# Half of the attention weights turned by VectorE and DMA, and every engine in the order of the source

## The chip, the cores and the metric

One Trainium2 chip, one of its cores. The metric is the device time of one launch in microseconds (us). A profile is one more execution, recorded instruction by instruction. The engines: TensorE (PE in the profile, its weight loads PEld), VectorE (DVE), ScalarE (ACT), GpSimd (POOL), and SyncE (SP), which here only issues DMAs.

## The reference

One block of a hybrid encoder: 512 tokens of width 2048, all in float32. Cut to what matters here:

```python
mod = silu(c) @ w_cond + b_cond                       # shift, scale, gate
h = rms_norm(x) * (1 + scale) + shift
proj = h @ w_in                                       # 2048 x 7200
aq, ak, av, ag, gq, gk, gv, gg, lr_f, lr_b = split(proj)
# attention, 16 heads of 64; three dilated windows (128,1), (512,4), (2048,16),
# merged by their softmax denominators, a shared T5 bias on the logits
a_out = merged_attention(aq, ak, av, rel_bias) * silu(ag)
# gated linear attention, 4 heads, forward and backward scans summed
g_out = rms_norm(o_fwd + o_bwd) * gla_norm_gain * silu(gg)
x = x + gate * (concat(a_out, g_out) @ w_out)
return rms_norm(x) * final_gain
```

For one head the three windows merge into one softmax over all 512 keys, with one bias row by distance (it holds the log of how many windows contain a key). So P, the weights of a head, is a 512 x 512 matrix, made in four tiles of 128 queries x 512 keys. The product with the values needs it with the keys on the partitions: each tile has to be turned.

## The kernel before

Each float32 operand is split into a high part (rounded to the float32r that TensorE takes) and a low part (the rest). `three` sums three products: high by high, high by low, low by high. ScalarE makes the high part (`split_hi`, `act(hi, raw)`), VectorE the low one (`split_lo`, `tt(lo, raw, hi, subtract)`).

After a first stage (condition sums, norm, the value columns `sa` and the columns `sb`) the projection runs in units of 512 columns, in the order qk2, qk4, qk6, gk, gv0, gv1, ag0, ag1, gg0, gg1, o0 to o3. A unit has eight weight groups of 256 rows (512 KB each, tile `raw`, four buffers). A group is loaded two or three ahead and split one ahead (tiles `whi` and `wlo`, three buffers each). The unit has four PSUM tiles `ps_...`, out of five buffers, and each group gives six matmuls to each of them. The unit's progress is counted in ticks: three matmuls are a tick, 64 ticks a unit.

Beside a unit's matmuls runs side work, put at places that are shares of the ticks. In qk2, qk4, qk6 and gk this is `attention` of four heads (two pairs) each. For each of a head's four tiles of queries:

- `score`: two matmuls (PSUM `s`), on VectorE the sum with the bias row and the minimum (tile `p`), on ScalarE the exponential with the row sum, on VectorE the reciprocal of the sum (`st`), on POOL the scaling of `p`.
- `turn`: four TensorE transposes into PSUM `t`, then high part (ScalarE) and low part (VectorE) into `pt`.
- `values`, for two tiles (a half of the head's queries) together: eight matmuls with the value tiles `vv`, PSUM `o`; ScalarE copies one half (`oh`), VectorE adds the other into `cat`.

At the end of qk2, qk4 and qk6 `qk_evict` takes four PSUM tiles into the operands of the next four heads: `qs` and `ks` (high part by ScalarE, low part by VectorE, in each of two halves), `kl`, and DMAs that copy `ks` and `kl` to the other 64 partitions. It is written behind the unit's loop, ahead of the next unit.

Other side work are sums of 1024 columns on VectorE (`rawv` for a bias row of the values, `rawg` for the gate), each with a load of 512 KB. `SUMS_IN` says how many go into which unit.

TensorE executes in the order of the source. ScalarE, VectorE, POOL and SP are ordered by the framework's scheduler from the first `qk_evict` on; there the side work is marked urgent. Semaphores tie the engines together, and each engine takes its own list in order.

## Time and profile before

| | us |
|---|---|
| median of three runs | 958.55 |
| the three runs | 958.09, 958.55, 958.55 |
| the profiled execution | 959.9 |
| its span, first to last instruction | 957.9 |
| TensorE busy in the span | 939.7 |
| VectorE, ScalarE, POOL busy | 605.3, 431.5, 81.1 |
| start of the units qk2, qk4, qk6, gk, gv0 | 191.9, 257.3, 323.7, 390.3, 457.5 |

The profiled execution lies 1.35 us over the median; 2.0 us of it are outside the span. Matmuls are pipelined, so that a row's duration is longer than the step from one to the next: what a matmul costs is read from the starts of its neighbours. A row in the timeline gives start, duration, engine, line, operation, out<-in, and in brackets the idle time ahead of it with what ended that.

### The profile page before, as it was taken

How to read it: one execution, taken by the hardware profiler on the slowest of the kernel's cores; microseconds unless marked ns; L12 is line 12 of the kernel's file. 1: busy time of each engine (PE TensorE's matmuls, PEld its weight loads, DVE VectorE, ACT ScalarE, POOL GpSimd, SP SyncE). 2: the span in 40 equal slices, each digit the busy share in tenths (PEclk: the TensorE clock that was granted, in tenths of full speed). 3: DMA queues.
4: the chain of work that ended last, by engine and by line, in shares of the span. 5: the costliest groups of instructions: out<-in, count | busy, mean ns of one | idle time of the engine just before them, and what ended most of it. 6: DMA issues, size and time to landing. Idle time of an engine off the chain costs nothing.

```text
span 957.9 us, 11999 instructions
## 1 busy us (share of the span) xinstructions
PE 939.7 (98%) x4464; PEld 777.1 (81%) x4464; DVE 605.3 (63%) x900; ACT 431.5 (45%) x719; POOL 81.1 (8%) x100
## 2 busy tenths in 40 slices
PE   8999999999999999999999999999999999999996
PEld 5888788888888888888778888888887888888884
DVE  7988899675756676766435656675964352546421
ACT  5443533565655655655215544543834152233222
POOL 0000000012122022122000000000010000202120
PEclk9999999999999999999999999999999999999998
DMA  9999687443333463533454244354555464244013
GB/s 330 413 411 365 229 296 275 150 131 105 112 103 105 144 200 108 173 127 103 150 176 146 86 132 154 132 176 154 173 195 183 132 221 154 92 151 152 23 55 121
DMA packets 45180, 163.76 MB, mean 171 GB/s; under 512 B 5730, under 2 KB 6018, under 8 KB 40386
## 3 DMA queue, kind: packets, MB, share of 16 engines
q1 hardware_dynamic: 44946, 162.68, 49.9%
q8 instruction: 35, 0.57, 0.2%
q10 hardware_dynamic: 176, 0.33, 0.1%
q14 instruction: 23, 0.18, 0.1%
HBM read 154.51 MB, written 4.28 MB: 166 GB/s over the span
## 4 chain that ended last, share of the span: by engine, by line
PE 84%; DMA 6%; DVE 5%; issue 3%; ACT 1%; SPq 0%; POOL 0%; ACTq 0%; DVEq 0%; POOLq 0%
PE ps_o L170 6%; PE ps_o L169 6%; PE ps_o L171 6%; DMA rawg<-in_wg 6%; PE ps_qk L170 5%; PE ps_qk L169 5%; PE ps_qk L171 5%; PE o L611 3%; PE sta L169 3%; PE sta L170 3%; PE sta L171 3%; PE stb L171 3%; PE stb L169 3%; PE stb L170 3%; PE ps_gv L171 3%; PE ps_gv L170 3%
## 5 line engine op out<-in xcount | busy, mean ns | idle before, releaser
L585 POOL TENSOR_SCALAR p<-p,st 128x512 f32<-128x512 f32 x64 | 45.5, 711 | 406.6 <-DVE st L584 357.9
L244 DVE CUSTOM_DVE_ANT_0 cb<-cb,sb,c_bcond 128x2048 f32<-128x2048 f32 (+1 forms) x32 | 73.4, 2294 | 0.0
L583 ACT ACTIVATE p<-p,st 128x512 f32<-128x512 f32 x64 | 46.1, 721 | 56.8 <-DVE st L580 56.3
L602 DVE TENSOR_TENSOR pt<-t,pt 128x512 fp32r<-128x512 f32 x64 | 44.0, 689 | 16.2 <-ACT pt L601 15.8
L580 DVE CUSTOM_DVE_ANT_0 p<-s,g 128x512 f32<-128x512 f32 x64 | 43.6, 687 | 14.8 <-PE s L577 14.5
L601 ACT ACTIVATE pt<-t 128x512 fp32r<-128x512 f32 x64 | 37.8, 592 | 10.2 <-PE t L597 9.2
L244 DVE CUSTOM_DVE_ANT_0 rawg<-rawg,sb,gate 128x1024 f32<-128x1024 f32 x16 | 20.5, 1283 | 29.6 <-DMA rawg<-in_wg 29.6
L611 PEld LDWEIGHTS o<-pt,vv 128*128 128x128 f32 x256 | 34.7, 188 | 5.0 <-DVE pt L602 2.2
L597 PEld LDWEIGHTS t<-c_ident,p 128*128 128x128 f32 x256 | 31.8, 140 | 8.5
L597 PE MATMUL t<-c_ident,p 128*128 128x128 f32 x256 | 38.3, 272 | 0.0
L611 PE MATMUL o<-pt,vv 128*128 128x256 f32 x256 | 36.6, 283 | 0.9 <-DVE pt L602 0.8
L244 DVE CUSTOM_DVE_ANT_0 rawg<-rawg,sb,c_bcond 128x1024 f32<-128x1024 f32 x16 | 20.5, 1283 | 26.3 <-DMA rawg<-in_wg 26.3
L1014 POOL TENSOR_TENSOR x<-x,fgain 128x512 f32<-128x512 f32 x12 | 20.3, 1696 | 185.3 <-ACT ysq L1012 185.3
L1012 ACT ACTIVATE ysq<-x 128x512 f32<-128x512 f32 x16 | 10.1, 632 | 47.2 <-DVE x L1010 47.2
L767 POOL TENSOR_SCALAR dc<-st,sc 128x256 f32<-128x256 f32 x16 | 10.4, 652 | 245.5 <-DVE st L764 240.6
L1009 DVE TENSOR_TENSOR y<-ps_o,sb 128x512 f32<-128x512 f32 x16 | 10.9, 684 | 25.9 <-PE ps_o L171 25.9
L584 DVE RECIPROCAL st<-st 128x1 f32<-128x1 f32 x64 | 10.3, 162 | 24.9 <-ACT p L583 24.9
L576 PE MATMUL s<-ks,qs 128*128 128x512 f32 x64 | 25.1, 391 | 0.0
L577 PE MATMUL s<-kl,qs 128*128 128x512 f32 x64 | 25.0, 391 | 0.0
L774 ACT ACTIVATE sq<-st,sc 128x256 f32<-128x256 f32 x24 | 12.2, 509 | 26.8 <-DVE st L769 14.3
L1010 DVE TENSOR_TENSOR x<-y,x 128x512 f32<-128x512 f32 x16 | 18.0, 1125 | 0.3
L614 ACT ACTIVATE oh<-o 64x256 f32<-64x256 f32 x32 | 12.2, 382 | 13.0 <-PE o L611 12.2
(1275 smaller groups left out, 2916.7 us busy)
## 6 DMA issues: line engine op xcount, KB each, us to landing
cb<-in_wm SPq DMA_DIRECT2D x31, 1024.0 KB, 7.9
rawg<-in_wg SPq DMA_DIRECT2D x32, 512.0 KB, 3.4
raw_o<-in_w_o SPq DMA_DIRECT2D x32, 512.0 KB, 3.4
raw_qk<-in_w_qk SPq DMA_DIRECT2D x24, 512.0 KB, 3.4
rawb<-in_w_sb SPq DMA_DIRECT2D x16, 512.0 KB, 4.8
rawv<-in_wv SPq DMA_DIRECT2D x16, 512.0 KB, 3.8
raw_gv<-in_w_gv SPq DMA_DIRECT2D x16, 512.0 KB, 3.5
raw_ag<-in_w_ag SPq DMA_DIRECT2D x16, 512.0 KB, 3.3
```

Source lines behind the costliest of these rows:

```text
L169: mm(ps, lh, rh, start=first, stop=False)
L170: mm(ps, ll, rh, start=False, stop=False)
L171: mm(ps, lh, rl, start=False, stop=last)
L244: nc.vector.tensor_tensor_reduce(out=w, in0=w, in1=with_, op0=ALU.mult, op1=ALU.add, scale=1.0, scalar=init, accum_out=dst)
L576: mm(ps, qs[:, q], ks, start=True, stop=False)
L580: nc.vector.tensor_tensor_reduce(out=t, in0=ps, in1=gt[h][:, P * i:P * i + 512], op0=ALU.add, op1=ALU.min, scale=1.0, scalar=3e38, accum_o ...
L583: act(t, t, AF.Exp, bias=st[:, 0:1], scale=-1.0, accum_out=st[:, 1:2])
L585: nc.gpsimd.tensor_scalar(t, t, st[:, 2:3], 1.0, op0=ALU.mult, op1=ALU.mult)
L597: nc.tensor.transpose(pk[:, kt * P:kt * P + P], t[:, kt * P:kt * P + P], ident)
L601: act(hi, src, AF.Copy)
L602: tt(lo, src, hi.bitcast(F32), op=ALU.subtract)
L611: mm(po[:, :256], vv[h // 4][:, kt, h % 4, :], t[:, w, kt, :], start=kt == 0 and w == 0, stop=kt == 3 and w == 1)
```

## The change

1. For queries 0 to 255 of each head (half 0, `BY_DVE`), P is turned without TensorE. `turn` transposes the 128 x 512 tile in blocks of 32 x 32 on VectorE; `leave` writes it to DRAM from SP; `back` reads it in four DMAs of 32 partitions x 8 x 128 elements (runs of 512 bytes), so that the blocks land in their places; `part_hi` (ScalarE) and `part_lo` (VectorE) split 128 x 1024 at once. Half 1 keeps the TensorE transposes (`pe_turn`).
2. The units qk2 to gv0 stand in a manual schedule of ScalarE, VectorE, POOL and SP: the order is that of the source. Reciprocal and scaling are a step of their own (`scale`), and each step of a tile has its place, in tiles behind its score.
3. Ahead of qk4, qk6 and gk not one weight group is split in the unit before but two (of gk's follower gv0 still one), and these units take their first two groups together, PSUM tile by PSUM tile.
4. The loads of the weight groups of qk2 (from the fourth), qk4, qk6 and gk and of the bias rows `g` are issued by ScalarE and no longer by SP.
5. Eight sums move out of qk6 and gk into gv0, gv1, ag0 and gg1; the two small operands `lrs` are made in gk and not at the head of gv0.

```diff
-ATT_AT = (0.17, 0.8, 0.04, 0.05, 0.05)
+ATT_AT = (0.12, 0.057)
+BY_DVE = (0,)
+BACK_AT = (2.7, 4.1, 4.4, 5.6)
-SUMS_IN = {"qk6": 4, "gk": 4, "gv0": 9, "gv1": 2, "ag0": 7, "ag1": 9, "gg0": 9}
+SUMS_IN = {"gv0": 12, "gv1": 5, "ag0": 8, "ag1": 9, "gg0": 9}
...
-            nc.sync.dma_start(raws[i], a["w_" + u][g])
+            queue = nc.scalar if u[:2] in ("qk", "gk") and i > 2 else nc.sync
+            queue.dma_start(raws[i], a["w_" + u][g])
...
                 act(t, t, AF.Exp, bias=st[:, 0:1], scale=-1.0, accum_out=st[:, 1:2])
+                pr_[h, i] = t, st
+            return go
+
+        def scale(h, i):
+            def go():
+                t, st = pr_.pop((h, i))
                 nc.vector.reciprocal(st[:, 2:3], st[:, 1:2])
                 nc.gpsimd.tensor_scalar(t, t, st[:, 2:3], 1.0, op0=ALU.mult, op1=ALU.mult)
...
+        def turn(h, i):
+            def go():
+                t = T2(f"pt{h}{i}")
+                nc.vector.transpose(t.rearrange("p (b k r) -> p k b r", b=4, k=4), pr_.pop((h, i)))
+                pr_[h, i] = t
+        def leave(h, i):
+            def go():
+                half, ii = divmod(i, 2)
+                if ii == 0:
+                    away[h, half] = dp.tile([2, P, 512], F32, tag=f"away{h}{half}", name=f"away{h}{half}")
+                nc.sync.dma_start(away[h, half][ii], pr_.pop((h, i)))
+        def back(h, half):
+            def go():
+                t = away.pop((h, half))
+                f = RAW(f"pf{h}{half}", [8, 128])
+                for b in range(4):
+                    nc.sync.dma_start(f[32 * b:32 * b + 32], bass.AP(
+                        t.tensor, t.offset + P * b, [[512, 32], [32 * 512, 8], [1, P]]))
+                pf[h, half] = f
+        def part_hi(h, half):
+                ...
+                act(t[:, 0].rearrange("p k (b r) -> p k b r", b=8), src, AF.Copy)
+        def part_lo(h, half):
+                ...
+                tt(lo, src, hi.bitcast(F32), op=ALU.subtract)
...
-        for x in range(n + 4):
-            if x < n:
-                items.append(score(*tiles[x]))
-            if 2 <= x <= n + 1:
-                items.append(turn(*tiles[x - 2]))
-            if 3 <= x <= n + 2 and tiles[x - 3][1] % 2 == 1:
-                items.append(values(tiles[x - 3][0], tiles[x - 3][1] // 2))
+        for x in range(n):
+            h, i = tiles[x]
+            items.append((x, score(h, i)))
+            items.append((x + 0.75, scale(h, i)))
+            half, ii = divmod(i, 2)
+            if half in BY_DVE:
+                items.append((x + 1.1, turn(h, i)))
+                items.append((x + 1.5, leave(h, i)))
+                if ii:
+                    for at, piece in zip(BACK_AT, (back, part_hi, part_lo, values)):
+                        items.append((x + at, piece(h, half)))
+            else:
+                items.append((x + 1.8, pe_turn(h, i)))
+                if ii:
+                    items.append((x + 2.9, values(h, half)))
+        items.sort(key=lambda v: v[0])
+        start, step = ATT_AT
+        return [(start + step * x, go) for x, go in items]
...
+        steps = [order_[:2]] if name in ("qk4", "qk6", "gk") else [order_[:1], order_[1:2]]
+        for step in steps + [[g] for g in order_[2:]]:
             todo = []
             if 0 in tiles:
+                end = upto[name, step[-1]] + (name[:2] == "qk" and step[-1] == order_[-1])
+                todo = list(range(gi[name, order_[0]], end + 1))
...
             for n, i in enumerate(tiles):
+                for g in step:
+                    hi, lo = wts[gi[name, g]]
...
+    with tc.manual_schedule(engines=PLANNED):
...
+        for n, p in (("qk2", 0), ("qk4", 2), ("qk6", 4)):
+            ps = unit(n, False, attention((p, p + 1)) + ([(0.6, shift_row)] if p == 4 else []))
+            for q in range(2):
+                qk_evict(p + 2 + q, ps[2 * q], ps[2 * q + 1])
...
+        ps = unit("gv0", True, some_sums("gv0"), lr=lr_tick)
```

How the order moves at the border from qk2 to qk4. The names: `p33` is the tile of head 3's last 128 queries, `st33` its row sums, `t33` its transposes, `qk40` to `qk42` the first three weight groups of qk4 (`h` high, `l` low), `qs2.`, `kl2.`, `qs3.`, `kl3.` the results of the eviction. VectorE before:

```order
L297 TENSOR_TENSOR qk41l_2149<-raw_qk41_1961,qk41h_2148 128x1024
L584 RECIPROCAL st33_2037<-st33_2037 128x1
L602 TENSOR_TENSOR pt30_2004<-t31_2050,pt30_2004 128x4x128
L540 SCALAR_TENSOR_TENSOR qs20_2106<-ps_qk2_0_1509,qs20_2106 64x512
L602 TENSOR_TENSOR pt31_2061<-t32_2062,pt31_2061 128x4x128
L540 SCALAR_TENSOR_TENSOR qs21_2109<-ps_qk2_0_1509,qs21_2109 64x512
L618 TENSOR_TENSOR cat0_1549<-o30_2072,oh30_2081 64x256
L550 TENSOR_TENSOR kl20_2113<-ps_qk2_1_1510,ks20_2112 64x512
L602 TENSOR_TENSOR pt31_2061<-t33_2090,pt31_2061 128x4x128
```

VectorE after, at the same place:

```order
L302 TENSOR_TENSOR qk41l_1997<-raw_qk41_1924,qk41h_1996 128x1024
L545 SCALAR_TENSOR_TENSOR qs20_2077<-ps_qk2_0_1513,qs20_2077 64x512
L545 SCALAR_TENSOR_TENSOR qs21_2080<-ps_qk2_0_1513,qs21_2080 64x512
L555 TENSOR_TENSOR kl20_2084<-ps_qk2_1_1514,ks20_2083 64x512
L555 TENSOR_TENSOR kl21_2090<-ps_qk2_1_1514,ks21_2089 64x512
L545 SCALAR_TENSOR_TENSOR qs30_2095<-ps_qk2_2_1515,qs30_2095 64x512
L545 SCALAR_TENSOR_TENSOR qs31_2098<-ps_qk2_2_1515,qs31_2098 64x512
L555 TENSOR_TENSOR kl30_2102<-ps_qk2_3_1516,ks30_2101 64x512
L555 TENSOR_TENSOR kl31_2108<-ps_qk2_3_1516,ks31_2107 64x512
L302 TENSOR_TENSOR qk42l_2120<-raw_qk42_1999,qk42h_2119 128x1024
L594 RECIPROCAL st33_2070<-st33_2070 128x1
L612 TENSOR_TENSOR pt31_2138<-t32_2139,pt31_2138 128x4x128
```

The reciprocal of the last tile stood ahead of the eviction and now stands behind all eight pieces of it and the split of a weight group. TensorE before, with the last matmuls of qk2:

```order
L597 MATMUL t33_2090<-c_ident_1459,p33_2036 128x128 x4
L169 MATMUL ps_qk2_2_1511<-h_hi_150,qk27h_1958 128x512
L170 MATMUL ps_qk2_2_1511<-h_hi_150,qk27l_1959 128x512
L171 MATMUL ps_qk2_2_1511<-h_lo_151,qk27h_1958 128x512
L169 MATMUL ps_qk2_3_1512<-h_hi_150,qk27h_1958 128x512
L170 MATMUL ps_qk2_3_1512<-h_hi_150,qk27l_1959 128x512
L171 MATMUL ps_qk2_3_1512<-h_lo_151,qk27h_1958 128x512
```

TensorE after; the last matmuls of qk2 and six of qk4 stand ahead of these rows, and POOL's scaling of p33 must be done ahead of `t33`:

```order
L608 MATMUL t32_2139<-c_ident_1459,p32_2033 128x128 x4
L173 MATMUL ps_qk4_0_2115<-h_hi_150,qk41h_1996 128x512
L174 MATMUL ps_qk4_0_2115<-h_hi_150,qk41l_1997 128x512
L175 MATMUL ps_qk4_0_2115<-h_lo_151,qk41h_1996 128x512
L173 MATMUL ps_qk4_0_2115<-h_hi_150,qk41h_1996 128x512
L174 MATMUL ps_qk4_0_2115<-h_hi_150,qk41l_1997 128x512
L175 MATMUL ps_qk4_0_2115<-h_lo_151,qk41h_1996 128x512
L173 MATMUL ps_qk4_1_2116<-h_hi_150,qk40h_1993 128x512
L174 MATMUL ps_qk4_1_2116<-h_hi_150,qk40l_1994 128x512
L175 MATMUL ps_qk4_1_2116<-h_lo_151,qk40h_1993 128x512
L608 MATMUL t33_2155<-c_ident_1459,p33_2069 128x128 x4
```

The transposes of the last tile moved from nine matmuls ahead of the border to fifteen behind it. In the middle of qk4, at head 5, VectorE had before:

```order
L580 ISA p50_2294,st50_2295<-s50_2291,g5_2211 128x512
L580 ISA st50_2295 128x1
L584 RECIPROCAL st50_2295<-st50_2295 128x1
L602 TENSOR_TENSOR pt41_2303<-t42_2304,pt41_2303 128x4x128
L618 TENSOR_TENSOR cat0_1549<-o40_2314,oh40_2323 64x256
L580 ISA p51_2337,st51_2338<-s51_2334,g5_2211 128x512
```

And now:

```order
L583 ISA p50_2310,st50_2311<-s50_2307,g5_2207 128x512
L583 ISA st50_2311 128x1
L302 TENSOR_TENSOR qk44l_2318<-raw_qk44_2122,qk44h_2317 128x1024
L594 RECIPROCAL st50_2311<-st50_2311 128x1
L612 TENSOR_TENSOR pt41_2296<-t43_2331,pt41_2296 128x4x128
L583 ISA p51_2343,st51_2344<-s51_2340,g5_2207 128x512
L583 ISA st51_2344 128x1
L620 STREAM_TRANSPOSE pt50_2352<-p50_2310 128x4x4x32
L654 TENSOR_TENSOR pt40_2350<-pf40_2289,pt40_2350 128x1024
```

New on VectorE are the 32 x 32 transposes and the split of 1024 columns of the returned half; gone are the two splits of 512 columns per head that followed TensorE's transposes of half 0.

More of the change, by code (lines that the diff above doesn't have):

```diff
@@ L587, in score, with pe_turn @@
             return go
[L589 removed]
+        def pe_turn(h, i):
             def go():
@@ new lines, in unit @@
+                for g in step:
+                    hi, lo = wts[gi[name, g]]
+                    for kk in range(2):
+                        k = 2 * g + kk
+                        rh, rl = (h_hi[:, k, :], h_lo[:, k, :]) if rhs is None else rhs[k]
+                        first, last = (g, kk) == (order_[0], 0), (g, kk) == (order_[-1], 1)
+                        if natural:
+                            t = slice(i * P, i * P + P)
+                            cw = slice(kk * 512, kk * 512 + 512)
+                            three(ps[n], rh[:, t], rl[:, t], hi[:, cw], lo[:, cw], first, last)
+                        else:
+                            c = slice(kk * 512 + i * P, kk * 512 + i * P + P)
+                            three(ps[n], hi[:, c], lo[:, c], rh, rl, first, last)
+                        tick += 1
+                        if tick % (2 * len(tiles)) == 2:
+                            for i_ in todo:
+                                if i_ <= upto[name, step[-1]]:
+                                    split_lo(i_)
+                        while pos < len(side) and side[pos][0] * ticks <= tick:
+                            urgent(side[pos][1])
+                            pos += 1
+                    if lr is not None:
+                        lr(4 * g + i)
```

107 lines of the change are left out of this document (44 added, 63 removed).

## The prediction

> **What bounds the kernel now.** I read the page's engine table first, then what TensorE waits for, then the units as windows.
>
> ```profile
> PE 939.7 (98%) x4464; PEld 777.1 (81%) x4464; DVE 605.3 (63%) x900; ACT 431.5 (45%) x719; POOL 81.1 (8%) x100
> ...
> PE pc L238 <- ACT c L236: 3.4, 1, 3.4
> PE gn L819 <- ACT gsh L817: 1.2, 1, 1.2
> PE go L805 <- DVE at L791: 1.0, 1, 1.0
> PE o L611 <- DVE pt L602: 0.8, 1, 0.8
> ...
> 191.90:257.30 65.40, 65.37 (x346) 54.89 (x345) 43.50 (x90) 38.81 (x75) 11.15 (x16) 1.00 0.37 113
> 257.30:323.70 66.40, 66.37 (x353) 55.90 (x352) 41.93 (x89) 37.43 (x72) 11.17 (x16) 1.00 0.36 108
> 323.70:390.30 66.60, 66.57 (x355) 55.89 (x354) 47.24 (x100) 37.60 (x73) 11.13 (x16) 1.00 0.51 162
> 390.30:457.50 67.20, 66.36 (x353) 55.91 (x352) 44.98 (x94) 36.50 (x70) 12.05 (x16) 1.00 0.42 132
> ```
>
> TensorE is busy in 98% of the span and has no wait of weight inside the four attention units (the last four rows: stretch, its length, then busy time of PE, PEld, DVE, ACT, POOL, granted clock, DMA share): 65.4 to 67.2 us each, TensorE idle for 0.03 us in three of them and 0.84 us in gk. So a matmul taken away here is time saved, and any wait put in is time lost, as TensorE has nothing to make it up with. VectorE has some 20 us to spare in a unit and ScalarE 28, but only if the order lets them use it.
>
> **What is removed from TensorE.** The chain of waits prices four transposes and eight value matmuls directly, and the timeline the step of a plain matmul:
>
> ```profile
> 204.27 0.44 PE t L597 x4
> 210.68 0.94 PE o L611 x8
> ...
> 207.54 0.39 PE L169 MATMUL ps_qk<-h_hi,qk22h 128*128 128x512 f32 x1
> 207.77 0.39 PE L170 MATMUL ps_qk<-h_hi,qk22l 128*128 128x512 f32 x1
> ```
>
> Four transposes cost 0.44 us, not the 0.60 us of their busy rows, and a matmul 0.23 us from start to start. Half of the 64 groups go: 32 x 0.44 = 14.1 us saved. A unit of 66.4 us becomes one of 62.9. TensorE's list is otherwise the same, in other places. The 0.84 us of gk go too, since `lrs` is now made earlier: 0.8 us.
>
> **The border: what is put in.** At the end of qk2, qk4 and qk6 the lists of VectorE and ScalarE now hold the whole eviction ahead of the last tile's reciprocal, and TensorE meets that tile's transposes 15 matmuls behind the border. The durations of that chain:
>
> ```profile
> 190.02 0.59 ACT L539 ACTIVATE qs<-stb 64x512 fp32r<-64x512 f32 x1
> 190.65 0.68 DVE L540 SCALAR_TENSOR_TENSOR qs<-stb,qs 64x512 fp32r<-64x512 f32 x1 [1.71 <-ACT qs L539]
> 191.37 0.59 ACT L539 ACTIVATE qs<-stb 64x512 fp32r<-64x512 f32 x1 [0.75 <-DVE qs L540]
> 191.99 0.69 DVE L540 SCALAR_TENSOR_TENSOR qs<-stb,qs 64x512 fp32r<-64x512 f32 x1 [0.66 <-ACT qs L539]
> 192.72 0.68 DVE L550 TENSOR_TENSOR kl<-stb,ks 64x512 fp32r<-64x512 f32 x1
> ...
> 248.92 1.06 ACT L313 ACTIVATE qk41h<-raw_qk 128x1024 fp32r<-128x1024 f32 x1 [0.95 <-PE ps_qk L171]
> 248.95 0.39 PE L577 MATMUL s<-kl,qs 128*128 128x512 f32 x1
> 249.49 0.69 DVE L580 CUSTOM_DVE_ANT_0 p<-s,g 128x512 f32<-128x512 f32 x1 [1.06 <-PE s L577]
> 250.10 1.22 DVE L297 TENSOR_TENSOR qk41l<-raw_qk,qk41h 128x1024 fp32r<-128x1024 f32 x1
> 250.22 0.73 ACT L583 ACTIVATE p<-p,st 128x512 f32<-128x512 f32 x1 [0.24 <-DVE st L580]
> 251.06 0.60 ACT L601 ACTIVATE pt<-t 128x512 fp32r<-128x512 f32 x1
> 251.24 0.16 DVE L584 RECIPROCAL st<-st 128x1 f32<-128x1 f32 x1
> 251.56 0.70 POOL L585 TENSOR_SCALAR p<-p,st 128x512 f32<-128x512 f32 x1 [4.16 <-DVE st L584]
> ```
>
> The first five rows show that the two engines alternate on one PSUM tile: ScalarE's second half waits for VectorE's first (0.75 us idle), and the next tile's low part starts 192.72 - 190.65 = 2.07 us behind this one's. Four tiles take 0.63 + 3 x 2.07 + 1.34 + 0.69 = 8.87 us from ScalarE's first start to VectorE's last end; ScalarE ends at 8.15. Let s be the start of VectorE's minimum for the last tile. Exponential after 0.73, ScalarE free after another 0.84: the eviction starts at s + 1.57. Behind it come the high part of the third group (1.06), the low part (1.14 from start to start, handover 0.03), the reciprocal, then POOL 0.32 later for 0.70 us: 8.15 + 1.06 + 0.03 + 1.14 + 0.32 + 0.70 = 11.40. So `t33` can start at s + 12.97.
>
> When is s? Let T be the border on TensorE. The last score's second matmul starts four matmuls ahead of T (0.92 us), and the minimum starts 0.54 us behind that start (248.95 to 249.49): s = T - 0.38 at the earliest. In the last 12 us ScalarE has, between two exponentials, three splits of 1024 columns in a row (1.06 us each); adding up both engines' rows in their new order from head 3's first score, I get the minimum 0.9 us late, s = T + 0.5. TensorE reaches `t33` at T + 15 x 0.23 + 0.44 = T + 3.9. It waits 13.5 - 3.9 = 9.6 us there; 8.7 with s at its earliest. Behind `t33` stand, on TensorE, all of qk4; behind the reciprocal, on VectorE, the splits of half 1 and the returned half, whose users TensorE meets 2 us and more later, so they add nothing. Three such borders: 28.8 us, bounds 26.1 and 35 (s 3 us late).
>
> Before, the reciprocal (251.24) started 1.75 us behind the minimum, six us ahead of the border.
>
> The Trainium skill, "TensorE: Matmul & The Clock Gate", section "Architectural detail: the array is 16× 32×32, not 1× 128×128", says that ScalarE and VectorE take their queue strictly first in, first out, so that a ready reciprocal can't pass a waiting eviction. By that rule the wait stands as worked out; were it false, the sum would be that of the first rival. No run here shows it as yet.
>
> **The border to gv0.** Here ScalarE evicts alone, and one split follows:
>
> ```profile
> 187.59 2.35 ACT L439 ACTIVATE gqt<-stb 128x512 f32<-128x512 f32 x4
> ...
> rawv<-in_wv SPq DMA_DIRECT2D x16, 512.0 KB, 3.8
> ```
>
> Four copies take 2.43 us (to the next ScalarE row, 190.02). s + 1.57 + 2.43 + 1.06 + 0.03 + 1.14 + 0.32 + 0.70 = s + 7.25, T + 7.75; TensorE comes to `t153` at T + 15 x 0.23 + 0.44 + two matmuls for `lrs` (0.46) = T + 4.3: 3.4 us, bounds 2.5 and 5.4. Then VectorE has a sum ahead of the split that the last values need, and its load can be issued only when a `raw` buffer is freed, near T + 6; with 3.8 us to land and 1.28 for the sum the values wait 1.5 us more (bounds 0 and 3).
>
> **Inside the units.** VectorE gets 32 transposes. No row shows one; the nearest are a low part from PSUM and the slowest operation on 128 x 512, a scan:
>
> ```profile
> L602 DVE TENSOR_TENSOR pt<-t,pt 128x512 fp32r<-128x512 f32 x64 | 44.0, 689 | 16.2 <-ACT pt L601 15.8
> L717 DVE TENSOR_TENSOR_SCAN b<-rst,g x4: 1224/1225/1226, 523.1 to 680.6; 128x512 f32<-128x512 f32 x4
> L618 DVE TENSOR_TENSOR cat<-o,oh 64x256 f32<-64x256 f32 x32 | 13.3, 416 | 7.3 <-ACT oh L614 6.8
> L614 ACT ACTIVATE oh<-o 64x256 f32<-64x256 f32 x32 | 12.2, 382 | 13.0 <-PE o L611 12.2 <-ACT p L583 0.4
> ```
>
> I take 0.69 us, as the low part is like it in shape and also makes one result of each element; bounds 0.61 and 1.23. That is 8 x 0.69 = 5.5 us a unit, less 0.6 us for splits in one piece and 5 us for four sums that leave qk6 and gk: VectorE's busy time stays at 47 to 49 us of 63. What counts is the chain, since in a fixed order each engine waits for the other. For head 5 (its rows stand under the change): minimum to exponential 0.72, exponential and sum 0.83, high part 1.06, low part 1.15 + 0.03, reciprocal 0.15, low part of `t43` 0.61, so that the second minimum starts at 4.5 us; again 0.72 + 0.83, `part_hi` 1.06, `part_lo` 1.18, reciprocal and sum 0.5, third minimum at 8.8; 0.72 + 0.83, the copy and sum of values 0.76, reciprocal 0.14, the wait for the next group's high part and its low part 1.7, fourth at 13.0; 0.72 + 0.83, high and low part of `t52` 1.2: head 6 starts at 15.8 us. For head 6, where the groups fall otherwise, the same sum gives 14.1. TensorE's pace is 4 x 0.057 x 62.9 = 14.3 us a head. So half of the heads run late by up to 1.5 us, half catch up; TensorE meets the lateness at the values of half 0, which need `part_lo` (8.9 us behind the head's first score, when `part_lo` ends 9.0 us behind it: no slack). Each border lets the lists catch up, so for the twelve heads that aren't first in a unit I take 4 us in all; bounds 0 and 12 x 1.5 = 18.
>
> **The round trip by DRAM**, and SP:
>
> ```profile
> out<-x SPq DMA_DIRECT2D x16, 256.0 KB, 2.6
> ks<-ks SPq DMA_DIRECT2D x16, 128.0 KB, 2.2
> c_ident<-in_ident SPq DMA_DIRECT2D x1, 64.0 KB, 4.2
> ...
> 510.60 0.92 ACTq L946 DMA_DIRECT2D rst<-in_rst  x1
> 510.87 0.58 ACT L930 ACTIVATE gv<-ps_gv 128x512 f32<-128x512 f32 x1
> ```
>
> Per head two writes of 256 KB (2.6 us to landing) and four reads of 128 KB. With 0.47 us for each issue and 2.2 us (wide rows) to 4.2 us (512-byte rows) for the last read the trip takes 0.5 + 2.6 + 1.9 + 2.2 to 4.2 = 7.2 to 9.2 us behind the transpose; `part_hi` is reached some 10 us behind it. Hidden, with 1 to 3 us of cover; if that is gone ScalarE stands still with the exponentials behind it. SP's list at a border has the eight copies of `ks` and `kl` ahead of the reads, which then come at T + 12; their values are met only at T + 20, as TensorE waits at `t33` meanwhile. Some 16.8 MB more move, 10% of the 163.8, where DMA is busy 36 to 51%: nothing. Loads issued by ScalarE: in the one row the next activation starts 0.27 us behind the issue, while the one before still runs; 45 issues fall mostly where ScalarE waits: 0, at most 0.4 us each. The eight moved sums land in units where VectorE has over 10 us to spare: 0. The second group split ahead takes the buffers' third place and hides two splits at the border, which would stand in the chain otherwise; it brings no gain against before, where nothing waited.
>
> **Sum.** -14.1 - 0.8 + 28.8 + 3.4 + 1.5 + 4 = +22.8 us. Against the profiled execution 959.9 that is 982.7; it lay 1.35 over the median, and against 958.55 it is 981.4. I take 981.
>
> **Rivals.**
> - *Faster: the borders cost nothing.* If the eviction ran beside the last tile's reciprocal rather than ahead of it, TensorE would find `p33` scaled, as it did before. For it: the profile shows no wait of TensorE at the old borders, and VectorE's share is below 80%. Against: its list has the reciprocal behind the eviction. Without the 32.2 us of the borders: 949. It decides from a border wait of 3.1 us on: below, the change is faster.
> - *The transposes are slow.* At the scan's 1.225 us the chain of each head grows by 2 x 0.54 us; heads that had none to spare pass it on to TensorE, 12 x 1.07 = 13 us: 994. The Trainium skill, "VectorE: DVE Perf Modes", section "The three transpose paths", has 311 ns for 128 x 128 in two-byte elements, an estimate of 1.24 us for a tile of four such blocks; that is this case, and no trace here shows it.
> - *The round trip is late.* From 10 us on each further us stops ScalarE once per head; 1 us late in 16 heads is 16 us: 997.
> - *The borders cost half* (4 to 5 us), because the lists run ahead there or the eviction is quicker alone than beside other work: 967.
>
> **Chances.** The forecast, borders of 8 to 11 us with small change inside, 0.65; slow transposes 0.13; late trip 0.08; half borders 0.08; no border wait 0.06. A measurement of this kernel can tell 0.2%, 1.9 us, from no change. Only the last case is faster (0.06); no change lies between the last two (0.01); slower 0.93. The range, 967 to 998, takes in the half borders, the slow transposes and the late trip, and the bounds 8.7 and 11 of the border; the forecast's own is 972 to 990.
>
> **What would show it.** Right: TensorE waits at line 608 for POOL three times for 8 to 11 us, once for 2 to 5, and the reciprocal's row stands some 10 us behind its minimum there; the four units take 62 to 66 us of TensorE work each. Wrong: no wait of TensorE over 2 us at these borders (then it is faster); a DVE transpose over 0.9 us; `part_hi` waiting for DMA; waits at line 665 for `part_lo` of over 10 us in all.

## The result, and the profile after

The changed kernel takes 991.1 us, median of 4 runs (988.87 to 992.15), against 958.32 us (956.86 to 958.55, 4 runs) beside it: 1.0342 times as long, 95% interval 1.0322 to 1.0363. The profiled execution took 988.87 us, 987.0 us of it span; before it was 959.9 and 957.9. One of the four executions with one group at a time (below) took 1582.47 us at a granted clock of 0.559, and that run's time is that of the other three.

The page's engine table, and then the four attention units as windows (stretch, its length, busy time of PE, PEld, DVE, ACT, POOL with the number of instructions, granted clock, DMA share, GB/s), both of the changed kernel:

```profile
PE 934.1 (95%) x4336; PEld 768.6 (78%) x4336; DVE 621.5 (63%) x917; ACT 428.4 (43%) x704; POOL 80.0 (8%) x100
...
192.60:257.40 64.80, 62.18 (x297) 51.07 (x296) 39.94 (x83) 31.89 (x60) 9.95 (x15) 0.97 0.59 174
257.40:332.50 75.10, 65.02 (x321) 53.78 (x320) 45.67 (x93) 36.72 (x68) 11.14 (x17) 0.95 0.53 151
332.50:407.80 75.30, 65.22 (x323) 53.85 (x322) 45.76 (x93) 36.90 (x69) 11.23 (x17) 0.95 0.60 165
407.80:483.00 75.20, 64.90 (x321) 53.71 (x320) 45.68 (x93) 36.40 (x69) 10.90 (x16) 0.95 0.50 144
```

Where units of 66.4 to 67.2 us stood, three of 75.1 to 75.3 stand now. In each of them TensorE is idle for 10 us, and its granted clock is 0.95, not 1.00. The waits of TensorE (us in total, times, longest) name the places:

```profile
PE t L608 <- POOL p L595: 27.3, 8, 7.8
PE o L665 <- DVE st L583: 3.7, 3, 1.3
...
PE kt L804 <- DVE ki L794: 1.8, 1, 1.8
PE ps_qk L173 <- ACT qk22h L318: 1.6, 1, 1.6
```

The transposes of each unit's last tile wait three times some 7.8 us for POOL's scaling; the other five waits of that line are 1.84 us or less. This is the border from qk2 to qk4 in TensorE's timeline, with two later rows (start, length, operation, what ended the idle time; the new unit's first matmul is at 257.43):

```profile
261.29 0.50 PE L173 MATMUL ps_qk<-h_hi,qk40h 128*128 128x512 f32 x1 [0.51 <-DVE qs L545]
...
270.09 1.11 PE L608 MATMUL t<-c_ident,p 128*128 128x128 f32 x4 [7.84 <-POOL p L595]
...
273.13 0.57 PE L175 MATMUL ps_qk<-h_lo,qk41h 128*128 128x512 f32 x1
273.55 0.39 PE L173 MATMUL ps_qk<-h_hi,qk41h 128*128 128x512 f32 x1
...
280.18 1.19 PE L665 MATMUL o<-pt,vv 128*128 128x256 f32 x8 [1.16 <-DVE st L583]
...
289.68 0.65 PE L608 MATMUL t<-c_ident,p 128*128 128x128 f32 x4 [0.58 <-POOL p L595]
...
490.02 0.66 PE L608 MATMUL t<-c_ident,p 128*128 128x128 f32 x4 [1.84 <-POOL p L595]
```

Four costs stand in it: 0.51 us for the first bank's eviction, 7.84 us for the scaling, matmuls at steps of 0.42 us for 0.23 until 273.55 (1.6 us lost), and 1.16 us at the values of head 3's half 0, the returned one. Together that is 11.1 us. Of the last two rows, the first is one more wait, in the new unit's first head, and the second is the border to gv0, 7.0 us behind that unit's start (483.0). The other engines at the border to qk4:

```profile
256.95 0.69 DVE L583 CUSTOM_DVE_ANT_0 p<-s,g 128x512 f32<-128x512 f32 x1
...
257.73 0.72 ACT L586 ACTIVATE p<-p,st 128x512 f32<-128x512 f32 x1 [1.25 <-issue]
...
258.57 0.59 ACT L544 ACTIVATE qs<-ps_qk 64x512 fp32r<-64x512 f32 x1
...
259.20 0.69 DVE L545 SCALAR_TENSOR_TENSOR qs<-ps_qk,qs 64x512 fp32r<-64x512 f32 x1 [0.23 <-ACT qs L544]
...
259.92 0.59 ACT L544 ACTIVATE qs<-ps_qk 64x512 fp32r<-64x512 f32 x1 [0.75 <-DVE qs L545]
...
266.80 0.69 DVE L555 TENSOR_TENSOR kl<-ps_qk,ks 64x512 fp32r<-64x512 f32 x1 [0.66 <-ACT ks L553]
...
267.88 1.23 DVE L302 TENSOR_TENSOR qk42l<-raw_qk,qk42h 128x1024 fp32r<-128x1024 f32 x1 [0.39 <-ACT qk42h L318]
...
269.03 0.16 DVE L594 RECIPROCAL st<-st 128x1 f32<-128x1 f32 x1
...
269.34 0.69 POOL L595 TENSOR_SCALAR p<-p,st 128x512 f32<-128x512 f32 x1 [11.45 <-DVE st L594]
...
277.10 1.06 ACT L647 ACTIVATE pt<-pf 128x1024 fp32r<-128x1024 f32 x1 [5.27 <-DMA pf<-away]
...
278.20 1.22 DVE L654 TENSOR_TENSOR pt<-pf,pt 128x1024 fp32r<-128x1024 f32 x1 [5.64 <-ACT pt L647]
```

The exponential is done at 258.5, and its reciprocal comes at 269.03: between them stand, on VectorE, eight pieces of the eviction in step with ScalarE, and the split of `qk42`. Behind that both engines stand for over 5 us at the returned half, which hasn't landed before 277.10; the values at 280.18 need it, and the next tile's minimum stands behind it on VectorE. The new operation itself and its returning data are in the page's groups:

```profile
L620 DVE STREAM_TRANSPOSE pt<-p 128x512 f32<-128x512 f32 x32 | 22.7, 710 | 1.6 <-POOL p L595 1.5
...
L654 DVE TENSOR_TENSOR pt<-pf,pt 128x1024 fp32r<-128x1024 f32 x16 | 19.6, 1226 | 30.5 <-ACT pt L647 30.5
...
L647 ACT ACTIVATE pt<-pf 128x1024 fp32r<-128x1024 f32 x16 | 16.8, 1049 | 18.3 <-DMA pf<-away 18.3
```

A turn takes 0.71 us. ScalarE stands 18.3 us in all at returned halves that haven't landed, and VectorE 30.5 us behind ScalarE.

### The profile page after: what moved, and what is told of

Same layout as the page of the kernel before. It is cut to its first block, busy times and chain, and to the rows that moved or that the text cites. A ratio compares the mean times of both kernels' runs of the same rounds, so it can differ in the third digit from the quotient of the medians.

```text
span 987.0 us, 11869 instructions
## 1 busy us (share of the span) xinstructions
PE 934.1 (95%) x4336; PEld 768.6 (78%) x4336; DVE 621.5 (63%) x917; ACT 428.4 (43%) x704; POOL 80.0 (8%) x100
## 4 chain that ended last, share of the span: by engine, by line
PE 42%; DVE 8%; DMA 7%; ACT 4%; issue 4%; POOL 0%; ACTq 0%; SPq 0%; DVEq 0%; POOLq 0%
PE ps_o L175 6%; PE ps_o L173 6%; PE ps_o L174 6%; DMA rawg<-in_wg 3%; PE ps_gg L175 2%; PE ps_gg L173 2%; PE ps_gg L174 2%; DMA rawv<-in_wv 2%; PE ps_gv L174 2%; PE ps_gv L173 2%; PE ps_gv L175 2%; DMA pf<-away 1%; PE go L864 1%; PE ps_ag L175 1%; PE ps_ag L173 1%
## 5 line engine op out<-in xcount | busy, mean ns | idle before, releaser
L608 PE MATMUL t<-c_ident,p 128*128 128x128 f32 x128 | 21.0, 289 | 27.3 <-POOL p L595 27.3
L608 PEld LDWEIGHTS t<-c_ident,p 128*128 128x128 f32 x128 | 16.1, 147 | 33.9 <-POOL p L595 30.8
L654 DVE TENSOR_TENSOR pt<-pf,pt 128x1024 fp32r<-128x1024 f32 x16 | 19.6, 1226 | 30.5 <-ACT pt L647 30.5
L612 DVE TENSOR_TENSOR pt<-t,pt 128x512 fp32r<-128x512 f32 x32 | 22.0, 686 | 14.4 <-ACT pt L611 14.3
L647 ACT ACTIVATE pt<-pf 128x1024 fp32r<-128x1024 f32 x16 | 16.8, 1049 | 18.3 <-DMA pf<-away 18.3
L611 ACT ACTIVATE pt<-t 128x512 fp32r<-128x512 f32 x32 | 19.1, 596 | 12.4 <-PE t L608 11.6
L620 DVE STREAM_TRANSPOSE pt<-p 128x512 f32<-128x512 f32 x32 | 22.7, 710 | 1.6 <-POOL p L595 1.5
L833 ACT ACTIVATE sq<-st,sc 128x256 f32<-128x256 f32 x24 | 12.2, 509 | 25.4 <-DVE st L828 13.7
```

Of the source, the lines that this page charges most:

```text
L608: nc.tensor.transpose(pk[:, kt * P:kt * P + P], t[:, kt * P:kt * P + P], ident)
L620: nc.vector.transpose(t.rearrange("p (b k r) -> p k b r", b=4, k=4), pr_.pop((h, i)))
```

## The experiments

Theory 1: the lists in source order make the border, and the rest of the change does what it says. Rivals: the turning by VectorE and DMA gives back what it takes off TensorE (late halves); TensorE's lower clock behind the stall makes the time; the split of a third group ahead does. The 12 runs were made in three sets of four, each beside runs of the kernel before (medians 958.83, 958.07 and 957.72 us), and each ratio is to these.

**The reciprocal earlier.** The unit's last tile gets its scaling ahead of the eviction:

```diff
-            items.append((x + 0.75, scale(h, i)))
+            items.append((x + (0.4 if x == n - 1 else 0.75), scale(h, i)))
```

> The reciprocal and the scaling of a unit's last tile are put ahead of the eviction; nothing else is moved. Theory 1 (the eviction holds everything written behind it, not the reciprocal alone): the wait at t33 goes, but the splits of pt31 still stand behind the eviction and the third group's split; by the changed kernel's rows the last one ends near T + 13.0, and TensorE comes to the values o31 at T + 7.5, so a wait of some 5.5 us takes its place there: 11 us a border become 8, the time about 980 (976 to 984). Theory 2 (only the reciprocal counts): the border is free, 33 us go, about 958.

Measured: 997.25 us, ratio 1.0405 (1.0385 to 1.0426): above both expectations, and slower than the changed kernel. TensorE's waits in it:

```profile
PE o L665 <- DVE st L583: 12.9, 3, 5.4
PE o L665 <- DVE pt L612: 12.3, 4, 4.1
...
PE t L608 <- POOL p L595: 1.9, 1, 1.9
```

The wait of the transposes is gone, as the edit says (27.3 to 1.9 us), and the time with it is not: the values of half 1 now wait for their low part, which still stands behind the eviction (4.06 us at the first border, where 5.5 were expected), and the values of half 0 behind that (5.37 us), which was not expected. These wait for the returned half: SP issues its four reads behind the eviction's eight copies, from 268.70 on, and ScalarE stands for 9.01 us until they have landed, at 278.44. In the whole run ScalarE waits 30.0 us for returned halves, for 18.3 in the changed kernel. The wait named in the prediction was the first of several, and the late half is the next.

**TensorE kept busy.** 30 matmuls without use stand ahead of the border transposes, so that TensorE has no long idle time:

```diff
+                if i == 3 and h in (3, 7, 11):
+                    for z in range(30):
+                        mm(pk, h_hi[:, z % KT, 0:P], h_hi[:, z % KT, :], start=True, stop=True)
```

> 30 matmuls of 128x512 whose result is overwritten (6.9 us at 0.23 us each) stand ahead of the last tile's transposes at the three borders; they fit into the wait of 7.8 us. Theory 1 (TensorE runs at a lower granted clock for a few us because it stood idle: 0.69 in the 4 us behind the wait, 1.6 us lost each time): the clock stays near 1.0 there and 4 to 5 us go, about 986. Theory 2 (the slow steps behind the wait have another cause, the DMA traffic or the eviction): the time stays at 991 or grows by what of the matmuls doesn't fit.

Measured: 991.12 us, ratio 1.0337 (1.0316 to 1.0358): the changed kernel's time. The mean granted clock rose from 0.984 to 0.994, so the clock does go with TensorE's idle time, but the time stayed. Its waits (line numbers are 3 higher):

```profile
PE o L668 <- DVE st L583: 9.0, 3, 3.4
PE t L611 <- POOL p L595: 6.3, 7, 1.8
```

Behind the border transposes matmuls step by 0.23 us again, and what they gained is waited for at the next values, those of the returned half. So the clock is no cause of its own at the border; ScalarE's and VectorE's lists, and the half's landing, set when it ends.

**All tiles turned by TensorE**, in the new order:

```diff
-BY_DVE = (0,)
+BY_DVE = ()
```

> The order of the source, but all of P is turned by TensorE. Theory 1 (TensorE's list is 14.1 us longer, the borders stay as they are, about 3.5 us of waits for the late returned half go): about 1000 (995 to 1004). Theory 2 (turning by VectorE and DMA makes the order so full that it costs as much as it saves): within 3 us of the changed kernel's 991.

Measured: 997.12 us, ratio 1.0397 (1.0377 to 1.0417), in the range of theory 1: 6 us above the changed kernel, where the transposes alone are 14.1 us more of TensorE's work. The transposes wait as long as before (29.3 us in 5 waits, 7.8 us the longest), the values not at all. So the borders don't come from the turning by VectorE.

**One group at a time.** The two-group step and the third split ahead are undone:

```diff
-        steps = [order_[:2]] if name in ("qk4", "qk6", "gk") else [order_[:1], order_[1:2]]
+        steps = [order_[:1], order_[1:2]]
...
-                end = upto[name, step[-1]] + (name[:2] == "qk" and step[-1] == order_[-1])
+                end = upto[name, step[-1]]
```

> Part 3 alone is undone: each unit goes through its weight groups one at a time and splits no third group ahead; all else is as in the changed kernel (991.1). Theory 1 (the border is a backlog of ScalarE and VectorE, and what stands ahead of the third border transpose, the split of a third group included, sets it): without that split, 1.06 us on ScalarE and 1.23 us on VectorE, each of three borders is shorter by about 2.3 us: 991.1 - 3 x 2.3 = 984 (981 to 987), and the wait of the border transposes falls from 7.8 to about 5.5. Theory 2 (the eviction of the four banks itself sets the border, and the two-group step is what lets TensorE go on while banks are still being read): the new unit wants its second to fourth banks after 6 matmuls each, 1.4 us, instead of 2.8 us, so TensorE waits for the banks instead, some 4 us at each border: 991 + 3 x 4 = 1003 (997 to 1008), with waits at the projection's matmuls.

Measured: 1000.09 us (996.0 to 1001.01), ratio 1.0425 (1.0396 to 1.0454): theory 2 by its time. Its waits:

```profile
PE t L608 <- POOL p L595: 28.8, 8, 5.7
PE ps_qk L173 <- DVE qs L545: 3.8, 2, 1.9
...
PE ps_gk L173 <- DVE qs L545: 1.9, 1, 1.9
```

The longest wait falls from 7.8 to 5.7 us, as theory 1 has it for the missing split, but TensorE also waits 1.9 us for the banks three times, about half of the 4 us a border that theory 2 had, and the transposes' waits keep their sum. This part of the change helps by 9 us.

**No source order.** The units' instructions are left to the scheduler, which may put an engine's work in another order than the source:

```diff
-    with tc.manual_schedule(engines=PLANNED):
+    if True:
         for i in range(3):
             fetch(i)
```

> Half of P is still turned by VectorE and DMA, and the groups are still split two ahead, but VectorE, ScalarE, POOL and SP get their order from the framework's scheduler as before. Theory 1 (the order is the whole loss, turning by VectorE saves 14 us of TensorE): 944 to 949. Theory 2 (the new work on VectorE, or the round trip by DRAM, costs TensorE what it saves, whatever the order): 955 or more, with waits of TensorE for the returned half spread over the four units.

Measured: 963.56 us (10 runs), ratio 1.0052 (1.0033 to 1.0070): 27.5 us less than in source order, but not below the kernel before, so on theory 2's side. The border's waits for POOL are gone; the returned halves are waited for instead:

```profile
PE o L665 <- ACT pt L647: 6.7, 4, 2.5
PE o L665 <- DVE pt L654: 5.4, 8, 0.9
```

By this run alone the rival, that the turning gives back what it gains, had as much for it as theory 1. Two runs tell them apart.

**No source order, all tiles turned by TensorE** (both edits above):

> The run without source order in the units (963.6), and besides it all tiles of probabilities turned by TensorE as before (no tile by VectorE). What is left of the change are the weights' loads by ScalarE's queue, the first groups split a unit ahead and the moved sums. Theory 1 (turning by VectorE and DMA gains TensorE its 14 us and hands most of it back as the 12.1 us that the values' matmuls wait for late halves): without it the 14.1 come back and the 12.1 go, 963.6 + 14.1 - 12.1 = 966 (961 to 969), and the values' matmuls wait no more than 2 us. Theory 2 (the turning does gain its 14 us and another part of the change costs as much): 963.6 + 14.1 = 978 (973 to 982). Theory 3 (the turning is at fault for more than it gains): 953 to 959, at or below the kernel before (958.8).

Measured: 972.95 us, ratio 1.0160 (1.0140 to 1.0179): at the lower edge of theory 2's range. The turning gains 9.4 us here (973.0 to 963.6), waits and all, and it is another part of the change that costs. TensorE's waits are no longer at the values:

```profile
PE s L580 <- DMA kl<-kl: 6.2, 3, 2.1
PE s L579 <- DMA ks<-ks: 4.8, 4, 1.9
```

The scores wait for the copies of the keys that the eviction sends. Why they come late here and hardly in the next run was not tried. `BACK_AT` has no effect when no tile is turned by VectorE, so this run is also what the next one is without the turning.

**No source order, the returned half used later:**

```diff
-BACK_AT = (2.7, 4.1, 4.4, 5.6)
+BACK_AT = (2.7, 5.5, 5.9, 7.5)
```

> The run without source order in the units (963.6), with the three pieces behind the returning read placed later: ScalarE's part at 5.5 tiles for 4.1, VectorE's at 5.9 for 4.4, the values at 7.5 for 5.6. Theory 1 (the values' matmuls, which waited 12.1 us there, are placed before their half can be back): these waits go below 3 us and the time is 963.6 - 9 to 12 = 952 to 955, faster than before (958.8). Theory 2 (the half is late because VectorE and ScalarE have no room for it, and a later place only moves the wait or holds buffers longer): 961 or more, with the same sum of TensorE's waits under other names.

Measured: 944.38 us (943.79 to 945.67), ratio 0.9857 (0.9842 to 0.9871): theory 1, and 8 us better than it said. This version beats both kernels, the one before by 1.4%. Its units qk4 and qk6 as windows, and a border in it, where qk4 starts at 252.47:

```profile
252.50:315.00 62.50, 62.50 (x322) 52.89 (x321) 45.63 (x93) 36.91 (x68) 13.90 (x16) 1.00 0.63 182
315.00:377.50 62.50, 62.50 (x322) 52.73 (x321) 44.79 (x93) 37.03 (x69) 15.67 (x16) 1.00 0.66 198
```

```profile
253.63 0.71 ACT L586 ACTIVATE p<-p,st 128x512 f32<-128x512 f32 x1
...
254.90 0.15 DVE L594 RECIPROCAL st<-st 128x1 f32<-128x1 f32 x1
...
255.09 0.69 DVE L545 SCALAR_TENSOR_TENSOR qs<-ps_qk,qs 64x512 fp32r<-64x512 f32 x1
...
255.15 0.69 POOL L595 TENSOR_SCALAR p<-p,st 128x512 f32<-128x512 f32 x1 [2.96 <-DVE st L594]
...
257.31 0.60 PE L608 MATMUL t<-c_ident,p 128*128 128x128 f32 x4
```

The reciprocal stands here ahead of VectorE's next eviction piece, 1.3 us behind its exponential's start, and the border transposes start without a wait. The eight pieces are spread from 251.16 to 263.90 among other work, and TensorE is never idle in qk4 and qk6.

Against this run the changed kernel's span is 43.1 us longer (987.0 to 943.9). TensorE's busy time is 934.1 against 924.6 us, so 33.6 of the 43.1 are idle time and 9.5 are longer busy time. Of that 4.9 us are the slow matmuls behind the three border waits (1.6 each). The rest was not taken apart; it isn't all the clock, since a row that ends ahead of a wait counts with its 0.39 us, where the next one would start 0.23 behind it. In the same way the run with early places, 963.7 - 943.9 = 19.8 us longer, has 930.9 - 924.6 = 6.3 us more busy time beside its 12.1 us of waits at the values: that is the part which theory 1's expectation left out.

**Source's order, the returned half used later** (the last edit alone):

> The changed kernel in its source's order (991.1), with the three pieces behind the returning read placed later, as in the run at 944.4 without source order (ScalarE's part at 5.5 tiles, VectorE's at 5.9, the values at 7.5). Theory 1 (two separate costs: the lists in source order at the borders, and late halves; in source order the second is only the 1.2 us that the first values of a unit wait, three times, and the returned half's pieces that hold up ScalarE and VectorE behind it): 991.1 - 3.5 to 8 = 983 to 988, the border transposes still waiting over 7 us for GpSimd's scaling. Theory 2 (a late half stands at the head of ScalarE's and VectorE's lists and by that holds up everything behind it, the border's backlog too): 970 or less, border waits under 4 us.

Measured: 991.12 us, ratio 1.0333 (1.0306 to 1.0360): above both expectations, no change. VectorE's border in it (TensorE's border is at 255.6):

```profile
256.62 1.23 DVE L654 TENSOR_TENSOR pt<-pf,pt 128x1024 fp32r<-128x1024 f32 x1 [0.79 <-ACT pt L647]
...
257.76 0.68 DVE L583 CUSTOM_DVE_ANT_0 p<-s,g 128x512 f32<-128x512 f32 x1
...
269.82 0.15 DVE L594 RECIPROCAL st<-st 128x1 f32<-128x1 f32 x1
```

The first unit ended 1.8 us earlier, but the later pieces now stand ahead of the last tile's minimum, at 257.76, 2.1 us behind the border instead of 0.5 ahead of it, and the reciprocal comes at 269.82. ScalarE waits only 0.9 us for returned halves in this run, for 18.3, and the 3.7 us of TensorE's waits at the values are gone. But the border transposes still wait 22.0 us, and others have come: 5.5 us for the low part of the second weight group at the head of qk4, qk6 and gk, and 2.3 us at the head of gv0. So in source order the later places trade waits for others. Later places together with the earlier reciprocal were not tried. With the two runs without it that makes four corners, in us:

| | used early | used later |
|---|---|---|
| source's order | 991.1 | 991.1 |
| scheduler's order | 963.6 | 944.4 |

**The eviction taken apart**, in source order: the first two banks leave during the unit's last group, the other two early in the next unit:

```diff
-    def qk_evict(p, psq, psk):
+    def evict_q(p, psq):
...
+    def evict_k(p, psk):
...
+            def done(b, ps, p=p, rest=rest):
+                go = lambda: (evict_k if b % 2 else evict_q)(p + 2 + b // 2, ps)
+                if b < 2:
+                    go()
+                else:
+                    rest.append((EVICT_AT[b - 2], go))
```

> The changed kernel (991.1), but with the eviction taken apart: each bank of a unit is a piece of its own, the first two go out during the unit's last weight group as soon as their last matmul is done, the last two are placed into the next unit at 0.02 and 0.08 of its length, and the reciprocal of a unit's last tile stands a little earlier (0.70 for 0.75 of a tile). Theory 1 (the border's 11 us come from the eight pieces of one eviction standing in a row on ScalarE and VectorE): the border loses most of its wait: 991.1 - 3 x (8 to 11) = 958 to 967, granted clock of the units back at 0.98 or more, no wait of a border transpose over 3 us. Theory 2 (the border is set by whatever is late there in turn, the returned half and the next tile's minimum among it, as the two runs suggest in which one wait was removed and the time stayed or rose): the waits come back at other lines and the time stays above 980.

Measured: 976.34 us, ratio 1.0183 (1.0161 to 1.0204): between the theories. The border transposes wait 12.9 us in 5 waits, for 27.3 in 8, and the three later units fall to 70.2, 71.1 and 72.2 us. So some 15 of the border's 33 us go when the eviction no longer stands in one piece; the edit also has the last tile's reciprocal a little earlier, at 0.70 of a tile for 0.75, and the two were not tried apart. The rest was not located further.

**The same, the returned half used later:**

> Source's order with the eviction taken apart (976.3) and, besides, the later places of the pieces behind the returning read. Theory 1 (the 12.9 us that the border transposes still wait in that run come from ScalarE and VectorE standing at a late half): 976.3 - 10 to 15 = 961 to 966. Theory 2 (they come from the order of the other pieces, the groups' splits and the remaining evictions): 973 or more, with the same waits for GpSimd's scaling. Theory 3 (source's order itself costs nothing once no list stands at a late item): down to the 944.4 of the run without source order.

Measured: 977.04 us, ratio 1.0195 (1.0167 to 1.0222): theory 2, no gain; the border transposes wait 18.8 us in 4 waits. Again the later places gain nothing while the order is the source's.

**All tiles turned by VectorE**, on the version at 944.4:

```diff
-BY_DVE = (0,)
+BY_DVE = (0, 1)
```

> The run at 944.4 (no source order, later places), with all tiles of probabilities turned by VectorE and DMA, not half of them: 32 groups of four transposes less for TensorE, 32 turns more for VectorE, 128 KB round trips twice as many. Theory 1 (TensorE still sets the units' time, VectorE at 66% has room): 944.4 - 14.1 = 930 (928 to 935). Theory 2 (VectorE, or the raw buffers that the returning reads share with the weights, become the limit): 940 or more, with waits at the values or at the weights' groups.

Measured: 981.52 us, ratio 1.0244 (1.0204 to 1.0284): theory 2, and far above its bound of 940.

```profile
PE o L665 <- DVE pt L654: 11.6, 12, 1.7
PE o L665 <- ACT pt L647: 11.4, 8, 2.3
PE s L579 <- DMA ks<-ks: 4.8, 2, 4.1
...
PE s L580 <- DMA kl<-kl: 2.5, 2, 2.2
```

23 us of waits at the values are back, and the copies of the keys, which share SP's queue with twice as many trips, come late. VectorE's busy share of the whole run is 66%, as in the run at 944.4, which speaks against its load as the limit. That it is the queue was argued from these rows alone.

**Three moved sums in the other value unit**, on the version at 944.4:

```diff
-SUMS_IN = {"gv0": 12, "gv1": 5, "ag0": 8, "ag1": 9, "gg0": 9}
+SUMS_IN = {"gv0": 15, "gv1": 2, "ag0": 8, "ag1": 9, "gg0": 9}
```

> The run at 944.4 (no source order, later places), with three of the moved sums put into the first value unit and not the second, which gets 2 of them as before the change, for 5. Theory 1 (the 1.7 to 2.5 us that the second value unit's transposes of ki wait in every run since the change come from the three sums added there): the wait goes, 944.4 - 1.7 = 942.7 (941.5 to 943.5). Theory 2 (the wait is of another cause): 944.4 within 1, the wait stays above 1 us.

Measured: 945.13 us, ratio 0.9861 (0.9844 to 0.9879), theory 2's time by theory 1's mechanism. The wait for `ki` is gone, and another of 2.9 us has come for it:

```profile
PE z L765 <- DVE ups L1019: 2.9, 1, 2.9
```

It is in gv1 too (508.18). So those three sums do make the wait for `ki`; that the same sums, now in gv0, make the other one was not traced.

## Why the prediction was right, point by point

It said 981 us, slower by the borders, in a range of 967 to 998; 991.1 came. That is just outside the forecast's own 972 to 990: the range held because it left room for slow transposes, which did not come, and for a late round trip, which came, but mainly at the borders. By the medians the change costs 32.8 us, 10 more than the sum's 22.8. The profiled pair differs by 29.0 us, as the profiled execution before lies 1.6 us over the median and the one after 2.2 us under it; the points below account for this pair. The windows from before to after: 0.7 us ahead of qk2, then qk2 -0.6, qk4 +8.7, qk6 +8.7, gk +8.0, gv0 +3.9, gv1 +2.0, ag0 0.0, ag1 -0.6, gg0 -2.1, and 0.5 behind it.

- **What is removed: right in size.** In the version at 944.4 TensorE is busy 924.6 us, 15.1 less than before, and the kernel is 13.7 us faster. The 14.1 us do not stand alone in that: without the turning the same version takes 973.0, 28.6 us more, as other waits come with it. The 0.84 us of gk went too, but not by `lrs`, which was made later, from 459.7 on: the wait was at values at 452.65, whose low part stood on VectorE behind a sum (450.72).
- **The border's chain: right in kind and nearly in size.** From ScalarE's first eviction piece (258.57) to the start of the transposes (270.09) it takes 11.52 us, where 11.40 were worked out. With T, as in the prediction, for the border on TensorE (257.43), the last minimum started at its earliest, T - 0.48, not T + 0.5, and TensorE arrived 0.9 us later than thought: a wait of 7.84 us, where 9.6 were taken and 8.7 was the lower bound. The sign of being right, three waits of 8 to 11 us, was missed by 0.16 us.
- **"So they add nothing": the step that failed.** The prediction let nothing follow behind the border's wait, neither from the splits of half 1 nor from the returned half. There were 1.16 us at the values of half 0, for the returned half, 1.6 us of matmuls at the lower clock, and 0.5 us ahead of the wait. The border was 11.1 us, not 9.6: 33.4 for 28.8 in all. Removing the 7.84 us alone gained nothing, as the first run shows, for behind it stand waits of nearly the same sum, 25.2 us at the values of both halves.
- **The Trainium skill's first-in, first-out rule** ("TensorE: Matmul & The Clock Gate", "Architectural detail: the array is 16× 32×32, not 1× 128×128"): the trace agrees. The reciprocal's input was ready at 258.5, and it ran at 269.03, behind the evictions; listed ahead of seven of the eight, in the run at 944.4, it ran 1.3 us behind its exponential's start. So the rival without border costs (949) is what the scheduler's order gives with the later places, 944.4; with the early ones it gives 963.6.
- **gv0: near by luck.** +3.9 us measured, 4.9 taken. But the transposes wait 1.84 us there, under the lower bound of 2.5, and the values not at all, where 1.5 us were taken. Some 1.8 us of the 3.9 are TensorE's own work: two groups of transposes and one of values more than before stand behind this border, at 0.44 and 0.94 us each. They are missing in qk2, so the kernel pays nothing for them; the sum had no term for that.
- **Inside the units: 4 us taken, for a reason that was not borne out.** They were to come from heads behind the first that run late, at the values of half 0. No such wait exists: from 290.0 to 332.5, in the middle of qk4, TensorE is busy for 42.50 of 42.50 us. By difference (the unit's growth, less its border, plus the 3.5 us saved, and in gk the 0.84) about 1.0 us remains in each of the three later units. Of that 0.58 us is the wait at 289.68, in the first head. Most of the rest is the end of the row ahead of each of the unit's four waits: 0.39 us long, where the next matmul would start 0.23 behind its start. That these 3 us come near the 4 taken is luck.
- **The turn: right** at 0.69 us, measured 0.71. The rival of slow transposes, and the estimate of 1.24 us from the Trainium skill's page "VectorE: DVE Perf Modes" ("The three transpose paths"), are ruled out by the 710 ns.
- **The round trip: "hidden, with 1 to 3 us of cover" was wrong.** ScalarE waited 18.3 us for returned halves, in five waits, and that was one of the prediction's own signs of being wrong. At a border the reads come as early as was said (T + 10.8 for T + 12), but they have landed only by T + 19.7, and TensorE pays 1.2 us three times at the values. The later places remove these waits and gain nothing in source order, since other waits come; in the scheduler's order the same early places cost 19 us.
- **Not foreseen:** 2.4 us of waits in qk2, where `qk22`'s splits stand behind the first exponential, with a granted clock of 0.97 in that unit, and 2.0 us in gv1 for `ki`, made by the moved sums, which were put at 0. ag1 and gg0 gave 2.7 us back.

## What to carry to other kernels

Where engines work through their lists in a fixed order, put no long block, such as an eviction of several tiles by two engines in turn, as one piece ahead of a short step that another engine waits for; and when such a wait is found, ask what stands late behind it, since taking away the first wait may only uncover the next. A step that takes work off the bound engine can hide its whole gain behind an order that came with it: change the order and the work apart, then try them together, as 991, 964 and 944 us are the same work. Data that goes out and returns needs its users placed behind its landing; here this gained 19 us in the scheduler's order and nothing in the source's, where other work was late at the same place.

## What the runs showed of the hardware

TensorE's granted clock falls with a stall: with 8 us of idle time the windows behind the border show

```profile
263.00:271.00 8.00, 0.91 (x5) 0.91 (x6) 5.05 (x8) 3.62 (x6) 0.69 (x1) 0.73 0.71 161
271.00:275.00 4.00, 4.00 (x14) 3.18 (x14) 0.69 (x1) 0.60 (x1) 0.00 (x0) 0.69 1.11 246
```

The clock stays low from 270.09 to 273.55, 3.5 us of work, and matmuls step by 0.42 us instead of 0.23. The Trainium skill, "TensorE: Matmul & The Clock Gate", section "What's actually happening", has half the clock after an idle window of about 3.4 us and the full one after about 3.4 us of work: the trace agrees. A DMA share of 1.11 falls in the same windows, but with TensorE kept busy matmuls at the same place step by 0.23 us and the kernel's mean clock rose by 0.010, so it is the idle time. In that run matmuls also step by 0.43 us behind a wait of 2.90 us at the values (281.02 to 282.30), which is shorter than the page's idle window; here the measurement decides. Each wait of 7.84 us brought 1.6 us of slower matmuls with it.

The four reads of a returning half behind a border, in SP's timeline:

```profile
268.24 3.85 SPq L638 DMA_DIRECT2D pf<-away  x4
```

They took 3.85 us from the first issue to the end of the last, where 0.47 us an issue, 1.9 us in all, had been taken. ScalarE could start on their data at 277.10, 8.9 us behind the first issue, where 1.9 + 2.2 to 4.2 us had been taken.
